# Three of the first eight loads of a channel shuffle issued by ScalarE in place of SyncE

## The chip, the cores and the metric

The kernel runs on one core of one Trainium2 chip. The metric is the device time of one execution in microseconds (us), as the median of several runs. Differences of a few tenths of a per cent need several rounds, and are given with a 95% interval.

In the profile, DVE is VectorE, ACT is ScalarE, SP is SyncE, and an engine's name with a q (ACTq, SPq) is its sequencer, which issues transfers and waits on semaphores. L54 is line 54 of the kernel. A transfer is issued when its engine's sequencer hands it over, and it lands when its data has arrived and its semaphore says so.

## The reference, cut to what matters

```python
batch, h, w, c = 16, 64, 64, 256          # x is float32: 67.11 MB
x = x.reshape(batch, h, w, groups, c // groups)    # groups = 8
x = x.transpose(0, 1, 2, 4, 3)
return x.reshape(batch, h, w, c)
```

Within each row of 256 channels an 8 x 32 matrix is transposed. Every byte is read once and written once, and nothing is computed.

## The kernel before

The 65,536 rows are cut into 22 tiles: 21 of 24 rows per partition (3 MB) and one of 8 rows (1 MB). Eight buffers hold whole tiles. SyncE issues all loads and ScalarE all stores. DVE shuffles a piece of 8 rows from the buffer to PSUM (a second on-chip memory), and ACT copies it back into the buffer.

```python
_SIZES = [24] * 20 + [8, 24]
_BUFS = 8
_PIECE = 8
# ... cut: pools (pool with _BUFS buffers, psum with 2), rows()
    ctx.enter_context(tc.manual_schedule(engines=None))
    first = 0
    for q in _SIZES:
        buf = pool.tile([P, biggest * c], F32, name="buf")
        nc.sync.dma_start(out=buf[:, : q * c], in_=rows(x_flat, first, q))
        for k in range(0, q, _PIECE):
            piece = buf[:, k * c : (k + _PIECE) * c]
            bounce = psum.tile([P, _PIECE * c], F32, name="bounce")
            nc.vector.tensor_copy(
                out=bounce.rearrange("p (i j g) -> p i j g", j=CPG, g=G),
                in_=piece.rearrange("p (i g j) -> p i j g", g=G, j=CPG),
            )
            nc.scalar.copy(out=piece, in_=bounce)
        nc.scalar.dma_start(out=rows(out_flat, first, q), in_=buf[:, : q * c])
        first += P * q
```

Two things follow from this code. A load of tile t + 8 waits until the store of tile t has landed, because it reuses its buffer. And all transfers, loads and stores alike, share eight semaphores ("slots" below), dealt out in turn when the program is built. The order is not that of the source lines; in the trace of before it begins with loads 0, 1, 2, store 0, load 3, store 1. So an issue also waits until the earlier transfer on its slot has landed, whichever engine issued that one.

Of the kernel before, what the change touches and what calls it, by code (L numbers as in the profile page):

```python
# [1 line left out]

# [4 lines left out]


F32 = mybir.dt.float32
P = 128  # L10

_SIZES = [24] * 20 + [8, 24]
_BUFS = 8

_PIECE = 8


@with_exitstack
def kernel(
    ctx: ExitStack,  # L20
    tc: tile.TileContext,
    x: bass.AP,
    groups: bass.AP,
    out: bass.AP,
):
    nc = tc.nc
    b, h, w, c = x.shape
    G = int(groups)
    CPG = c // G
    assert G * CPG == c  # L30
    assert sum(_SIZES) * P == b * h * w
    biggest = max(_SIZES)

    x_flat = x.rearrange("b h w c -> (b h w c)")
    out_flat = out.rearrange("b h w c -> (b h w c)")

    pool = ctx.enter_context(tc.tile_pool(name="pool", bufs=_BUFS))
    psum = ctx.enter_context(
        tc.tile_pool(name="psum", bufs=2, space=bass.MemoryType.PSUM)
    )  # L40

    def rows(flat, first, q):

        return flat[first * c : (first + P * q) * c].rearrange("(p f) -> p f", p=P)

    ctx.enter_context(tc.manual_schedule(engines=None))
    first = 0
    for q in _SIZES:
        buf = pool.tile([P, biggest * c], F32, name="buf")
        nc.sync.dma_start(out=buf[:, : q * c], in_=rows(x_flat, first, q))  # L50
        for k in range(0, q, _PIECE):
            piece = buf[:, k * c : (k + _PIECE) * c]
            bounce = psum.tile([P, _PIECE * c], F32, name="bounce")
            nc.vector.tensor_copy(  # L54
                out=bounce.rearrange("p (i j g) -> p i j g", j=CPG, g=G),
                in_=piece.rearrange("p (i g j) -> p i j g", g=G, j=CPG),
            )
            nc.scalar.copy(out=piece, in_=bounce)  # L58
        nc.scalar.dma_start(out=rows(out_flat, first, q), in_=buf[:, : q * c])  # L59
        first += P * q  # L60


# [1 line left out]
_INS = ['x', 'groups']  # L64
_OUTS = [((16, 64, 64, 256), 'float32')]

_NUMBERS = {'groups': 8}


# [26 lines left out]
```

## Time and profile before

| | before |
|---|---|
| time, median of 3 runs | 317.67 us (317.38 to 317.92) |
| span of the profiled run | 315.9 us |
| moved | 134.24 MB, mean 425 GB/s |
| DVE busy / ACT busy | 72% / 38% |

From the page of the kernel before: busy time by engine; then the span in 40 equal slices (7.9 us each), with the busy share of DVE, ACT and the DMA engines in tenths and the rate; then the issues, with the size of a transfer and the median time from issue to landing.

```profile
DVE 227.9 (72%) x64; ACT 120.3 (38%) x65; POOL 0.2 (0%) x4
DVE  0699999959587685957008986999970299999900
ACT  0354455525252424330015416545500444555420
DMA  8999999999999999999999999999999999999997
GB/s 296 439 442 380 436 429 433 433 439 433 423 442 433 426 442 426 426 442 426 433 436 427 433 436 436 433 426 437 433 423 448 423 429 444 429 423 433 439 432 302
...
buf<-in_x_dram SPq DMA_DIRECT2D x21, 3072.0 KB, 58.4
out_dram<-buf ACTq DMA_DIRECT2D x21, 3072.0 KB, 24.2
```

Read the DMA row first. It is 9 (90% or more) everywhere but in the first and last slice, while DVE and ACT have holes. The transfers are the limit. There is one dip in the rate, in the fourth slice (380).

The same by windows (us from the start; length; busy time of each engine; clock; DMA share; GB/s):

```profile
11.00:24.00 13.00, 12.95 (x4) 6.88 (x4) 0.00 (x0) 1.00 0.99 427
24.00:26.00 2.00, 2.00 (x2) 0.65 (x1) 0.00 (x0) 1.00 1.04 430
26.00:28.00 2.00, 2.00 (x1) 1.21 (x1) 0.00 (x0) 1.00 1.02 319
28.00:30.00 2.00, 2.00 (x2) 1.10 (x1) 0.00 (x0) 1.00 0.98 393
...
36.00:139.00 103.00, 81.89 (x23) 44.76 (x24) 0.00 (x0) 1.00 1.01 433
```

Loads alone (11 to 24 us) and loads with stores (36 to 139 us) move at the same rate. The dip falls on the first store, which the timeline shows being issued at 23.68 us (start, duration, engine, line; in brackets the idle time before, and what ended it):

```profile
11.05 21.36 DVE L54 COPY bounce<-buf 128x2048 f32<-128x2048 f32 x6 [11.05 <-DMA buf<-in_x_dram]
...
23.68 0.37 ACTq L59 DMA_DIRECT2D out_dram<-buf  x1
```

The waits of before (who waited for whom; us in total, times, longest) show the slots at work: four times ACT stood still because the store that it was to issue had to wait for a load that was far down the other queue.

```profile
ACT buf L58 <- DVE bounce L54: 115.3, 56, 5.6
ACT buf L58 <- DMA buf<-in_x_dram: 55.7, 4, 26.0
DVE bounce L54 <- ACT buf L58: 38.8, 4, 18.8
```

The packet records of the trace give the floor. Most packets carry 24,576 bytes and take 912 ns on one of 16 DMA engines. All packets together make 308.2 us (24 KB ones), 5.0 us (8 KB ones) and 0.4 us (the rest) per engine: 313.6 us of the 315.9 us span, which leaves 2.3 us, or 0.7%. Some packets overlap. Counted by how many of 16 were under way at each moment, 3.8 us were empty, 1.8 us of them before the first packets and another 1.8 us after the last: there is no hole of note in between.

### The profile page before, as it was taken

Reading aid. Unit: us, or ns where it says so; the run is one execution under the profiler, and the core shown is the slowest. Engines: PE = TensorE matmul, PEld = TensorE weight load, DVE = VectorE, ACT = ScalarE, POOL = GpSimd, SP = SyncE. Lnnn points to the kernel's source line nnn. Section 1 sums busy time; section 2 is a strip of 40 time slices with the busy share of each in tenths; the row PEclk is TensorE's granted clock in tenths of the full one; section 3 lists DMA queues with packets and bytes.
Section 4 is the critical chain, followed back from the end, with each engine's and each line's share of the span. In section 5 each row is a group of like instructions: output and inputs, shape, how many; then the busy total and the mean of one; then the engine's idle time right before and its main releaser. Section 6 shows DMA issues by size and latency. Waiting matters only on the chain.

```text
span 315.9 us, 289 instructions
## 1 busy us (share of the span) xinstructions
DVE 227.9 (72%) x64; ACT 120.3 (38%) x65; POOL 0.2 (0%) x4
## 2 busy tenths in 40 slices
DVE  0699999959587685957008986999970299999900
ACT  0354455525252424330015416545500444555420
POOL 0000000000000000000000000000000000000000
DMA  8999999999999999999999999999999999999997
GB/s 296 439 442 380 436 429 433 433 439 433 423 442 433 426 442 426 426 442 426 433 436 427 433 436 436 433 426 437 433 423 448 423 429 444 429 423 433 439 432 302
DMA packets 6338, 134.24 MB, mean 425 GB/s; under 512 B 704, under 2 KB 704, under 8 KB 704
## 3 DMA queue, kind: packets, MB, share of 16 engines
q1 hardware_dynamic: 3168, 67.11, 49.9%
q10 hardware_dynamic: 3168, 67.11, 49.4%
q14 instruction: 2, 0.02, 0.0%
HBM read 67.11 MB, written 67.11 MB: 425 GB/s over the span
## 4 chain that ended last, share of the span: by engine, by line
DVE 54%; another core or an unknown queue 23%; issue 8%; ACT 5%; DMA 3%; DVEq 1%; ACTq 0%
DVE bounce L54 54%; ACT buf L58 5%; DMA buf<-in_x_dram 3%; DVEq L91 1%; ACTq L59 0%; DVEq L54 0%; ACTq L58 0%
## 5 line engine op out<-in xcount | busy, mean ns | idle before, releaser
L54 DVE COPY bounce<-buf 128x2048 f32<-128x2048 f32 x64 | 227.9, 3636 | 72.6 <-ACT buf L58 38.8
L58 ACT COPY buf<-bounce 128x2048 f32<-128x2048 f32 x64 | 119.0, 1866 | 171.1 <-DVE bounce L54 115.3
L58 ACT ACT_TABLE_LOAD x1 | 1.3, 1283 | 11.1 <-DMA buf<-in_x_dram 11.1
L77 POOL MEMSET const-bfloat16-1.0<- 128x1 bf16 x1 | 0.1, 102 | 0.0
L77 POOL MEMSET const-uint8-127<- 128x1 uint8 x1 | 0.1, 101 | 0.0
L77 POOL MEMSET const-float32-0.0<- 128x1 f32 x1 | 0.1, 99 | 0.2 <-issue 0.2
L77 POOL MEMSET const-float32-1.0<- 128x1 f32 x1 | 0.1, 98 | 0.0
## 6 DMA issues: line engine op xcount, KB each, us to landing
buf<-in_x_dram SPq DMA_DIRECT2D x21, 3072.0 KB, 58.4
out_dram<-buf ACTq DMA_DIRECT2D x21, 3072.0 KB, 24.2
buf<-in_x_dram SPq DMA_DIRECT2D x1, 1024.0 KB, 46.0
out_dram<-buf ACTq DMA_DIRECT2D x1, 1024.0 KB, 15.8
```

What stands on the lines that cost most here:

```text
L54: nc.vector.tensor_copy(out=bounce.rearrange("p (i j g) -> p i j g", j=CPG, g=G), in_=piece.rearrange("p (i g j) -> p i j g", g=G, j=CPG),)
L58: nc.scalar.copy(out=piece, in_=bounce)
L77: nc = _bacc.Bacc("TRN2", target_bir_lowering=False, num_devices=1)
L91: with _tile.TileContext(nc) as tc:
```

## The change

The change starts two loads at once, from two engines, and takes three issues off SyncE. The loads of tiles 1, 3 and 5 go to ScalarE, ahead of its first store. The loop is rewritten so that a load can be issued eight tiles ahead.

```diff
+_ACT_LOADS = (1, 3, 5)
...
+    def load(t):
+        buf = pool.tile([P, biggest * c], F32, name="buf")
+        loader = nc.scalar if t in _ACT_LOADS else nc.sync
+        loader.dma_start(out=buf[:, : _SIZES[t] * c], in_=rows(x_flat, t))
+        bufs[t] = buf
 
     ctx.enter_context(tc.manual_schedule(engines=None))
-    first = 0
-    for q in _SIZES:
-        buf = pool.tile([P, biggest * c], F32, name="buf")
-        nc.sync.dma_start(out=buf[:, : q * c], in_=rows(x_flat, first, q))
+    for t in range(_BUFS):
+        load(t)
+    for t, q in enumerate(_SIZES):
+        buf = bufs.pop(t)
...  (copies as before)
-        nc.scalar.dma_start(out=rows(out_flat, first, q), in_=buf[:, : q * c])
-        first += P * q
+        nc.scalar.dma_start(out=rows(out_flat, t), in_=buf[:, : q * c])
+        if t + _BUFS < len(_SIZES):
+            load(t + _BUFS)
```

The rewriting itself is no part of what is tested. Built with `_ACT_LOADS = ()`, the changed file gives on SyncE, ScalarE and VectorE the same instructions with the same waits as the kernel before (a comparison of the built programs, not a timed run). So everything that differs comes from the three loads, including a new dealing of the semaphore slots.

More of the change, by code (lines that the diff above doesn't have):

```diff
@@ L40, with rows @@
     )
-    def rows(flat, first, q):
-        return flat[first * c : (first + P * q) * c].rearrange("(p f) -> p f", p=P)
+    first = [sum(_SIZES[:t]) * P for t in range(len(_SIZES))]
+    def rows(flat, t):
+        n = P * _SIZES[t] * c
+        return flat[first[t] * c : first[t] * c + n].rearrange("(p f) -> p f", p=P)
+    bufs = {}
+    def load(t):
[3 more added lines that the diff above has]
+        bufs[t] = buf
     ctx.enter_context(tc.manual_schedule(engines=None))
-    first = 0
-    for q in _SIZES:
-        buf = pool.tile([P, biggest * c], F32, name="buf")
-        nc.sync.dma_start(out=buf[:, : q * c], in_=rows(x_flat, first, q))
+    for t in range(_BUFS):
+        load(t)
+    for t, q in enumerate(_SIZES):
+        buf = bufs.pop(t)
         for k in range(0, q, _PIECE):
```

## The prediction

> **What bounds the kernel now.** The transfers. The page moves 134.24 MB at a mean of 425 GB/s; its DMA row reads 9 in every slice but the first (8) and last (7). DVE is busy 72%, ACT 38%: neither is the limit. By windows the rate is 427 GB/s with loads alone (11 to 24 us), 430 with loads and stores mixed (24 to 139): the mix makes no difference. The Trainium skill ("DMA: Bandwidth & Descriptors", Where 436 GB/s comes from) puts a fabric ceiling at 435 GB/s; this trace agrees, so the middle has nothing to gain. In the DMA records a 3 MB load alone takes 7.3 us (loads 1 and 2 land at 18.3 and 25.6 us). 42 full transfers and two of a third make 42.67 x 7.28 = 310.6 us; the span is 315.9. At most 3 to 5 us of start, end and one dip (slice 4: 380 GB/s, when the first store starts) are not transfer.
>
> **What the change does.** Bytes, copies (64 x 3.6 us on DVE, 64 x 1.9 us on ACT) and stores stay. Three of 22 load issues (0.33 to 0.65 us each on SP) move to ACT, which is idle then. Two queues now load at once. The skill (same page, Issuing engines are not separate DMA queues) says both run on the same 16 DMA engines and interleave, saving only issue time; the trace shows such sharing: from 36 to 160 us loads and stores land 14.5 us apart each, twice 7.3. So tiles 0 and 1 should land together at about 18 us (before: 11.0 and 18.3), 2 and 3 at 33, 4 and 5 at 47 (before: 53 and 68).
> - Cost: DVE starts at about 18 us, 7 us later. Store 0 is issued at about 31 us (23.7), queues behind load 5, and lands at about 62 us (44.1).
> - Gain: none for the DMA engines: eight buffers of loads keep both queues supplied in this phase.
> - Semaphores are dealt anew by program order. Before, store 9's issue waits for load 12 (ACT blocked 138.8 to 164.2 us) and store 15's until 248 us. Now most stores wait for the store four before. Both ACT blocks should vanish, loads and stores alternating evenly until about 250 us.
> - End: 64 DVE copies at 3.56 us need 228 us, so DVE could end by 246. Last load at about 270 us (287), last store issued near 291 us (302.5), landing near 314 us (314.9), queued behind others.
>
> Following the program's waits with these durations (7.28 us per tile alone, 14.55 shared, 3.55 and 1.9 us per copy) ends both kernels at the same time.
>
> **On the critical path:** almost nothing. The 7 us later start is absorbed by slack in DVE and ACT; the bytes set the end. What can differ is the cold start of two queues and the dip of about 1 us at the first store: within 1 us together.
>
> **Predicted: 317.4 us**, 8 in 10 within 316.0 to 318.8. Chances: faster by over 2% 1.5%, within 2% 96.5%, slower 2%.
>
> **To check in the profile:** DMA row still all 9, mean 424 to 427 GB/s; DVE idle before its first copy about 18 us; median load landing nearer 29 us (58.4), stores' longer (24); ACT's wait for loads (55.7 us) nearly gone.
>
> **What would make it wrong:** unequal sharing between two loading queues, so that tile 0 or 1 is late and a queue runs dry; two load streams reading below 427 GB/s; a store blocked by a load near the end, leaving one or two stores late with the DMA engines idle before them.

## The result, and the profile after

| | before | after |
|---|---|---|
| time, median of 6 runs each | 317.63 us (317.38 to 317.92) | 317.81 us (317.59 to 318.13) |
| ratio after / before | | 1.0006, 95% interval 0.9993 to 1.0019 |
| span of the profiled run | 315.9 us | 316.0 us |

Ratios here and below are the mean time of one kernel's fast runs over that of the other's fast runs of the same rounds, so they are not quite the ratio of the quoted medians. The two kernels take the same time.

The same lines of the page after:

```profile
DVE 227.7 (72%) x64; ACT 119.8 (38%) x65; POOL 0.2 (0%) x4
DVE  0079999998999998957668595949006999996000
ACT  0034555444555444251615244242006544554000
DMA  8999999999999999999999999999999999999997
GB/s 308 439 448 417 429 398 420 426 448 426 423 445 435 420 439 439 417 440 442 423 429 445 426 423 445 433 417 442 439 420 439 430 443 420 432 445 426 423 431 302
...
out_dram<-buf ACTq DMA_DIRECT2D x21, 3072.0 KB, 43.7
buf<-in_x_dram SPq DMA_DIRECT2D x18, 3072.0 KB, 28.9
buf<-in_x_dram ACTq DMA_DIRECT2D x3, 3072.0 KB, 31.3
```

Almost everything inside moved, and the DMA row did not. DVE starts one slice later and is then full for longer. The median store takes 43.7 us from issue to landing (24.2 before) and the median load on SyncE 28.9 us (58.4 before): transfers queue in other places, but the same engines serve them at the same rate.

```profile
24.00:44.00 20.00, 20.00 (x7) 10.67 (x6) 0.00 (x0) 1.00 1.01 433
44.00:46.00 2.00, 2.00 (x1) 0.52 (x1) 0.00 (x0) 1.00 1.11 393
46.00:48.00 2.00, 2.00 (x2) 1.79 (x1) 0.00 (x0) 1.00 0.83 246
48.00:50.00 2.00, 2.00 (x2) 0.32 (x2) 0.00 (x0) 1.00 1.15 492
...
54.00:139.00 85.00, 78.85 (x23) 41.61 (x23) 0.00 (x0) 1.00 1.01 433
```

Two queues that both load (24 to 44 us) move 433 GB/s; one that loaded alone moved 427 (11 to 24 us, before). The dip is still there; it has moved from 27 us to 47 us, with the first store. (A window counts a packet where it starts, and 2 us hold only two or three packets of an engine, so a window can read too high or too low, as 492 does.)

```profile
17.72 60.37 DVE L67 COPY bounce<-buf 128x2048 f32<-128x2048 f32 x17 [17.72 <-DMA buf<-in_x_dram]
...
30.35 0.35 ACTq L72 DMA_DIRECT2D out_dram<-buf  x1
```

The first copy starts 6.7 us later (17.72 against 11.05), and so does the first store's issue (30.35 against 23.68). The waits after:

```profile
ACT buf L71 <- DVE bounce L67: 80.5, 46, 2.3
ACT buf L71 <- DMA out_dram<-buf: 47.7, 7, 7.5
DVE bounce L67 <- ACT buf L71: 44.3, 9, 18.2
ACT buf L71 <- DMA buf<-in_x_dram: 25.8, 2, 21.4
```

ACT waits less for loads (25.8 us against 55.7) and now waits for earlier stores (47.7 us), since those hold most of the slots that its stores get. The landing records of the trace, side by side (us from the start):

| | before | after |
|---|---|---|
| tiles 0 and 1 land | 11.0, 18.3 | 17.7, 17.9 |
| tiles 2 and 3 | 25.6, 38.8 | 32.3, 32.5 |
| tiles 4 and 5 | 53.4, 67.9 | 47.2, 47.4 |
| store 0 issued, landed | 23.7, 44.1 | 30.4, 62.5 |
| last load landed | 287.0 | 276.3 |
| last store issued, landed | 302.5, 314.9 | 291.7, 315.0 |

The last store is issued 11 us earlier and lands at the same time, because it waits in the queue for the transfers ahead of it.

### The profile page after: what moved, and what is told of

It is laid out like the page before. It is cut to its first block, busy times and chain, and to the rows that moved or that the text cites. A ratio compares the mean times of both kernels' runs of the same rounds, so it can differ in the third digit from the quotient of the medians.

```text
span 316.0 us, 288 instructions
## 1 busy us (share of the span) xinstructions
DVE 227.7 (72%) x64; ACT 119.8 (38%) x65; POOL 0.2 (0%) x4
## 4 chain that ended last, share of the span: by engine, by line
another core or an unknown queue 28%; DMA 28%; DVE 26%; issue 6%; ACT 2%; DVEq 1%; SPq 1%; ACTq 0%
DVE bounce L67 26%; DMA buf<-in_x_dram 14%; DMA out_dram<-buf 14%; ACT buf L71 2%; DVEq L105 1%; SPq L56 1%; ACTq L72 0%; ACTq L71 0%
## 5 line engine op out<-in xcount | busy, mean ns | idle before, releaser
L71 ACT ACT_TABLE_LOAD x1 | 1.3, 1283 | 17.8 <-DMA buf<-in_x_dram 17.8
## 6 DMA issues: line engine op xcount, KB each, us to landing
out_dram<-buf ACTq DMA_DIRECT2D x21, 3072.0 KB, 43.7
buf<-in_x_dram SPq DMA_DIRECT2D x18, 3072.0 KB, 28.9
```

## The experiments

The theory: the DMA engines are busy from the first packet to the last, and the end is set by their 313.6 us of packets. The later start of the copies is real, but it is absorbed as long as some queue holds a transfer. Three rivals: (A) the choice of issuing engine has a cost which a gain of the new slots hides, or the reverse; (B) two issuing engines bring a gain of issue time; (C) the chain of copies, 54% of the chain of waits in the profile of before, carries a part of the end.

### All eight first loads on ScalarE

```diff
-_ACT_LOADS = (1, 3, 5)
+_ACT_LOADS = (0, 1, 2, 3, 4, 5, 6, 7)
```

> The change taken further: all eight first loads are issued by ScalarE, none by SyncE, so the first store queues behind all eight. Theory (the bytes set the end; whoever issues, some queue always has work): 317.6 us within 1, ratio to before 0.998 to 1.003; tile 0 lands at 11 us again, store 0 lands only near 69 us, and the last store is issued near 287 us. Rival A (who issues matters: it cost something that a gain of the new order of semaphores hid): over 319 us, because stores start 25 us later. Rival B (two issuing engines give a gain of issue time): slower than after by the issue time, about 1 us.

Measured: 317.88 us (317.82 to 318.07); ratio to before 1.0007 (0.9994 to 1.0019, five rounds). Store 0 was issued at 23.7 us and landed at 70.3 us, 26 us later than before, behind eight loads; the last store was issued at 288.9 us. None of it shows in the time, which speaks against rivals A and B.

### No copies at all

```diff
-        for k in range(0, q, _PIECE):
-            ...  (both copies)
         nc.scalar.dma_start(out=rows(out_flat, t), in_=buf[:, : q * c])
```

> The changed kernel without its copies on DVE and ACT: each tile is stored as it was loaded (wrong result on purpose; same bytes, same 44 transfers). Theory: 317.3 us within 1, as the transfers alone take this time. Rival C (the chain of copies carries part of the end, 54% of the chain of waits of before): at least 2% less, 311 us or under.

Measured: 317.02 us (316.94 to 317.73), the result wrong; ratio to before 0.9983 (0.9970 to 0.9995, five rounds). Taking away 228 us of DVE and 120 us of ACT work saves about half a microsecond. Rival C falls: the share of a group in the chain of waits tells through which instructions the chain was traced, not what it would save to remove them. The run is also a bound for the copies: in the order of after, these 44 transfers take 317.0 us with nothing beside them. It does not test other orders of the transfers; for those there is only the estimate from before, where packets filled all but 2.3 us of the span.

### Paying for the first store early

```diff
+    warm = once.tile([P, _WARM], F32, name="warm")     # _WARM = 256
+    nc.vector.memset(warm, 0.0)
+    nc.scalar.dma_start(
+        out=rows(out_flat, P * sum(_SIZES[:-1]), _SIZES[-1])[:, :_WARM], in_=warm
+    )
     first = 0
```

> The kernel before with one small store (128 x 1 KB of zeros, overwritten at the end by the last tile's own store) issued by ScalarE at the very start. Question: is the dip at the first store (313 GB/s from 26 to 28 us in the packet records of before) a cost of the first store as such, which can be paid while the start is slow anyway? Theory that it can: the dip near 27 us is gone and the time falls by 0.3 to 0.8 us (ratio 0.9975 to 0.999). Rival: the dip stays at the first large store, and the time is the same or 0.3 us longer for the 0.13 MB.

Measured: 317.96 us (317.88 to 318.26); ratio 1.0010 (0.9997 to 1.0024, five rounds). The small store landed by 13.9 us. The windows of this run show the dip where it was:

```profile
24.00:26.00 2.00, 2.00 (x2) 0.65 (x1) 0.00 (x0) 1.00 1.01 418
26.00:28.00 2.00, 2.00 (x1) 1.21 (x1) 0.00 (x0) 1.00 0.91 270
28.00:30.00 2.00, 2.00 (x2) 1.11 (x1) 0.00 (x0) 1.00 0.93 369
```

The rival was right: the dip belongs to the first large store, not to the first store as such. It is not a cold queue either. With all eight loads on ScalarE that queue had been loading for 60 us, and its windows still read 356 and 344 GB/s from 58 to 62 us, at the change from loads to stores. What causes the dip stays open. The packet records say only what it consists of: the DMA engines are not idle, but packets of the loads still under way take longer. In the kernel before, load packets that start from 26 to 28 us take 1.33 us on average, store packets beside them the usual 0.91 us. The packets lengthened in the dip add 0.8 us per engine before and 0.9 us after.

### How much delay is absorbed

If the theory holds, there must be a limit. Eight buffers hold 8 x 7.3 = 58 us of loads, so the DMA engines were expected to run dry when store 0 is issued later than about 60 us. Before the change it is issued at 23.7 us and after it at 30.4 us, so the changed kernel should have 7 us less to spare. The first DVE copy was therefore repeated 8 or 10 times more in each kernel (28 and 36 us, correct results):

```diff
-            nc.vector.tensor_copy(
+            for _ in range(_EXTRA + 1 if t == 0 and k == 0 else 1):    # _EXTRA = 8 or 10
+                nc.vector.tensor_copy(
```

(In the kernel before, the condition reads `first == 0 and k == 0`.)

> The kernel before, with the first DVE copy made eight extra times, so that all later copies and store 0 come 28 us later (store 0 issued near 52 us in place of 23.7). Theory: eight buffers hold 8 x 7.3 us of loads, which keep the DMA engines busy until about 60 us; as long as store 0 is issued before about 59 us nothing is lost: 317.6 us within 1. Rival C (the chain of copies carries the end): 28 us longer, or a good part of it.

> The changed kernel, with the same eight extra copies. Its copies start 6.7 us later, so store 0 is issued near 59 us, just past the end of the eight loads' data. Theory: 2 to 4 us longer than without, 320.5 us within 1.5: the slack of 36 us of before is 29 us here. Rival (the 7 us later start costs nothing in any way): the same as late8_before.

> The kernel before with ten extra copies, 35.6 us. Store 0 is issued near 59 us. Theory: 320.4 us within 1.5, like late8_after. Rival C: 35 us longer.

> The changed kernel with ten extra copies. Store 0 is issued near 66 us; the DMA engines stand idle for about 6 us more than in late10_before. Theory: 327.6 us within 1.5, 7.2 us more than late10_before, which shows the later start in full once the slack is used up. Rival: the same as late10_before.

| first copy repeated | order of before | order of after |
|---|---|---|
| 8 times more | 317.61 us, ratio to before 0.9999 (0.9984 to 1.0014), store 0 issued at 52.6 us | 320.98 us, 1.0101 (1.0085 to 1.0118), store 0 issued at 59.6 us |
| 10 times more | 321.30 us, 1.0112 (1.0097 to 1.0127), store 0 issued at 60.1 us | 327.02 us, 1.0295 (1.0279 to 1.0310), store 0 issued at 66.6 us |

In the order of before, 28 us of delay cost nothing that can be measured. The same 28 us in the changed order cost 3.4 us, and the two cells in which store 0 is issued at about 60 us agree within 0.4 us. So the later start uses up about 7 us of slack, and no other cost shows. (The slots are dealt differently in these runs too; no store at the holes described here waited for one.)

The cost in these two cells came about otherwise than expected, and the forecast of 2 to 4 us was met partly by luck. The loads had not run out when store 0 was issued: load 7 landed at 61.7 us in late8_after and at 62.2 us in late10_before, and packets went on without a hole until 68.4 us. The hole comes after store 0. Load 8 needs the buffer of store 0, which landed at 69.5 us (69.6 us in late8_after), and store 1 is only issued 10.7 us after store 0. In late10_before:

```profile
68.00:70.00 2.00, 2.00 (x2) 1.17 (x1) 0.00 (x0) 1.00 0.06 25
70.00:72.00 2.00, 2.00 (x1) 0.70 (x1) 0.00 (x0) 1.00 0.83 209
```

This hole is worth 2.1 us in both cells; longer load packets, as in the dip above, make about another 1 us. To leave no hole, store 1 would have to send packets by 68.4 us. The first packet of a store that found the DMA engines nearly empty came 0.9 us after its issue (store 0 in both runs with ten extra copies), so by an estimate store 0 must be issued by 68.4 - 0.9 - 10.7, or about 57 us. Measured is only that 52.6 us is early enough and 59.6 us is too late.

The difference in the last row is 5.7 us, where 7.2 were expected; store 0 itself is issued only 6.5 us later there. In the last cell the loads do run out before store 0. The windows show the DMA engines without work, with DVE busy throughout:

```profile
50.00:60.00 10.00, 9.93 (x4) 1.87 (x1) 0.00 (x0) 1.00 1.00 428
60.00:62.00 2.00, 2.00 (x2) 0.81 (x1) 0.00 (x0) 1.00 0.12 49
62.00:64.00 2.00, 2.00 (x1) 1.05 (x1) 0.00 (x0) 1.00 0.00 0
64.00:66.00 2.00, 2.00 (x2) 1.26 (x1) 0.00 (x0) 1.00 0.00 0
66.00:68.00 2.00, 2.00 (x1) 0.60 (x1) 0.00 (x0) 1.00 0.46 197
...
74.00:76.00 2.00, 2.00 (x2) 0.61 (x1) 0.00 (x0) 1.00 0.12 49
```

Taking each window's shortfall against 430 GB/s, the 2 us windows shown lack 1.8 + 2 + 2 + 1.1 + 1.8 = 8.7 us, against 9.4 us of added time. (By the packet records, the holes are 6.6 us before store 0 and 1.5 us after it.) This is what a real cost looks like in the DMA row; neither kernel of the change has such a window.

### The same change where copies are the limit

Two settings. First, every DVE copy is made twice (correct result), so that DVE needs about 456 us:

```diff
-            nc.vector.tensor_copy(
+            for _ in range(2):
+                nc.vector.tensor_copy(
```

> The kernel before with every DVE copy made twice (right result), so that DVE needs 455 us and bounds the kernel. Theory: 483 us within 3, DVE busy without a stop from 11 us.

> The changed kernel with every DVE copy made twice. Theory: the 6.7 us later start now stands on the critical path: 490 us within 3, 6 to 8 us more than twice_before (ratio 1.013 to 1.017). Rival (the change is neutral whatever bounds the kernel): the same as twice_before.

Measured: 484.14 us (483.95 to 484.25) in the order of before and 490.87 us (490.87 to 490.95) in that of after; DVE is busy 95% and 94%. The ratios to the kernel before, 1.5233 and 1.5448, differ by a factor of 1.014. The added 6.73 us are the later start of DVE, 17.7 against 11.0 us, which is the only wait of DVE in either run (twice_before, then twice_after):

```profile
DVE bounce L55 <- DMA buf<-in_x_dram: 11.0, 1, 11.0
```

```profile
DVE bounce L68 <- DMA buf<-in_x_dram: 17.7, 1, 17.7
```

Here the later start, which costs nothing above, costs its full length.

Second, from tile 8 on only 8 of 24 rows are loaded and stored, with all copies kept. The results are wrong, with parts of the output never written; 80 MB are moved, and DVE's 228 us are the larger need.

```diff
+        some = _SIZES[t] if t < _BUFS else min(_SIZES[t], _PIECE)
-        loader.dma_start(out=buf[:, : _SIZES[t] * c], in_=rows(x_flat, t))
+        loader.dma_start(
+            out=buf[:, : some * c], in_=rows(x_flat, t)[:, : some * c]
+        )
...  (from tile 8 on the copies read the first piece and write each of the three
...   in turn, and the store takes 8 rows)
```

> From tile 8 on only 8 of 24 rows are loaded and stored, with all copies kept (wrong result on purpose): 80 MB, DVE's copies are the larger need. Eight first loads all on SyncE, which is the order of before. Theory: stores from 24 us on take half of the engines while loads 3 to 5 are under way, so these land 14.5 us apart and DVE, which takes 10.7 us a tile, runs dry between 55 and 97 us: about 268 us within 5.

> The same with loads 1, 3 and 5 on ScalarE as in the change. Theory: stores queue behind load 5, so loads have the engines to themselves until 47 us, land 7.3 us apart on average, and DVE does not run dry after its later start until tile 6 or 7: about 258 us within 5, some 10 us less than few_before. Rival (only the later start counts): 7 us more than few_before.

> The kernel of few_after with all eight first loads on ScalarE: one engine issues them, as in few_before, but stores still queue behind them, and tile 0 has the DMA engines to itself. Theory (the 12 us of few_after come from loads going ahead of stores on one queue, and its start paid 7 us for sharing between tiles 0 and 1): 248 us within 3, some 7 us less than few_after and 19 less than few_before. Rival (loads from two engines at once are what gains): 267 us, like few_before.

| loads on ScalarE | time | tiles 3, 4, 5 land | DVE busy from 48 to 100 us |
|---|---|---|---|
| none (few_before) | 266.78 us (266.49 to 266.93) | 38.8, 53.3, 67.9 | 34.7 of 52 us |
| 1, 3, 5 (few_after) | 254.93 us (254.79 to 255.02) | 32.6, 47.4, 47.6 | 50.9 of 52 us |
| all eight (few_all_act) | 248.22 us (247.58 to 248.50) | 33.0, 40.3, 47.6 | 50.6 of 52 us |

DVE's row on the three pages, in this order (slices of 6.6, 6.3 and 6.2 us):

```profile
DVE  0399999996785509996999999999999999999990
```

```profile
DVE  0019999999998999999999999999999999999990
```

```profile
DVE  0199999999979999999999999999999999999990
```

The change gains 11.9 us (4.4%) here. It is not two engines loading at once that gains: with all eight loads on one engine the gain is 18.6 us (7.0%). What the two faster runs share is that stores stand behind loads in the same queue, so that the loads land earlier. In few_before, stores sit in a queue of their own and take every other packet from 27 us on, while DVE is still short of tiles. And splitting loads 0 and 1 over two queues costs a start: DVE's first copy begins at 17.8 us in few_after and at 11.1 us in few_all_act, and the two times differ by 6.7 us. One thing is not separated. In few_before DVE's hole has two sources, tiles that land late and ACT held up 16.9 us by a slot that load 7 held:

```profile
DVE bounce L75 <- DMA buf<-in_x_dram: 18.5, 3, 10.9
ACT buf L79 <- DMA buf<-in_x_dram: 16.9, 1, 16.9
DVE bounce L75 <- ACT buf L79: 12.0, 2, 9.8
```

After its start at 10.9 us, DVE thus waited 7.6 us for tiles and 12.0 us for ACT. Both waits shrink when the loads come earlier (in few_all_act, 1.4 us for ACT and none for tiles after the start), and no run took one away alone. So the order of the queue and the slots together gain 18.6 us; how much of it the order alone would gain is not shown.

## Why the prediction was right

Predicted were 317.4 us, and the measured median is 317.81 us.

- **What bounds the kernel.** Right. The transfers alone take 317.0 us (no copies).
- **Sharing of the DMA engines by two loading queues.** Right: tiles 0 and 1 were to land at about 18 us and landed at 17.7 and 17.9; tiles 2 to 5 came within 1 us of what was written. The Trainium skill ("DMA: Bandwidth & Descriptors", Issuing engines are not separate DMA queues) says that the issuing engine makes no difference to which DMA engines do the work; the rates of 427 GB/s with one loading queue and 433 GB/s with two agree with it.
- **The later start, and its absorption.** Right, and shown: it uses 7 us of a slack that by the estimate above is about 33 us before and 27 us after. The prediction called it slack in DVE and ACT and argued from the end ("DVE could end by 246"); it said that eight buffers of loads keep the queues supplied, but not for how long. That is where the limit lies: the first stores must follow so early, store 0 by about 57 us, that one of them is ready when the loads of eight buffers and store 0 are done.
- **"Both ACT blocks should vanish."** Wrong in part. The block at 138.8 to 164.2 us went, but store 15 still has a slot that a load holds (load 18, landed at 237.5 us), and ACT stood 21.4 us for it. The prediction read "most stores wait for the store four before" as "all until 250 us". ACT's wait for loads fell to 25.8 us, not to nearly nothing. It cost no time, as the DMA row stayed full.
- **Last load at about 270 us.** It landed at 276.3. The mis-sized term appears to be the 1 MB load of tile 20: a third of the prediction's 14.55 us for a shared tile would be 4.9 us, and it took 9.7 us after load 19 (252.0 to 261.8 us). The packet records show turns by packet, not by byte: from 252 to 260.2 us, 105 of its 8 KB packets (309 ns) start beside 111 of the stores' 24 KB packets (912 ns). An engine carries 8 of the load's packets, and 8 x (0.309 + 0.912) = 9.8 us. The Trainium skill (same page, Queues, rings and completion order) says that a DMA engine goes round its queues packet by packet; this trace agrees, with 9.7 us in the kernel before too (262.8 to 272.5 us).
- **The cold start and the dip, "within 1 us together".** Right: the first packet starts at 1.74 us in both kernels, and the dip moved with the first store and stayed.

## What to carry to other kernels

Look at the DMA row before anything else. Here it was full from the first slice to the last, and moving issues to another engine changed only where transfers wait. Then work out how much delay the buffers absorb (here eight loads of 7.3 us, less what it takes until the next store is ready), for this says when a later start begins to cost. Where copies are the limit instead, try the queue as a way to give priority: in the runs with fewer bytes it paid to put the first loads ahead of the stores on the stores' queue, and to let the first tile have the DMA engines to itself.

## What the Trainium skill lacked or had wrong

- "DMA: Bandwidth & Descriptors", Issuing engines are not separate DMA queues, says that issuing from several engines only saves issue time. For this kernel that held (ratio 1.0006). That section leaves out that the choice of queue orders loads against stores: with copies as the limit, runs of the same transfers took 266.8, 254.9 or 248.2 us (a new dealing of the slots included).
- The same page, Where 436 GB/s comes from, says that transfers between HBM (the chip's main memory) and SBUF (where the buffers lie) are bound at about 358 GB/s per core. Read alone this misleads; the note just above it on that page ties the figure to both cores of a pair streaming. On this core alone, loads with stores ran at 433 GB/s for over 80 us in both kernels, close to its other figure, the fabric ceiling of 435 GB/s.
- The same page says that queues take turns by packet, but not what follows for shares: a 1 MB load in 8 KB packets beside a store in 24 KB packets took 9.7 us where an equal share of bytes would give 4.9.
- No page read tells of the dip at the change from loads to large stores: 319 GB/s for 2 us in the kernel before, 246 in the one after. A small store ahead did not remove it. In the kernel before, load packets that start in those 2 us take 1.33 us on average, against 0.91 us.
